# Whole weight blocks in fixed places, and a ring for their parts, in a two-layer trunk

## The chip, the core and the metric

The kernel runs on one core of a Trainium2 chip. A core has TensorE (matrix products, into the banks of PSUM), VectorE and ScalarE (elementwise work), GpSimd (called POOL in the profile) and SyncE, which here only issues transfers. Each engine works through its own queue in order; semaphores tie the queues together. The metric is the device time of one execution in microseconds (us): 1143.61 us for the kernel before, the median of three runs (1143.24 to 1144.23).

## The reference, cut to what matters

Two layers with RMS norms, 256 positions, width 2048, all in float32:

```python
# layer 0, gMLP
proj = xn @ w_in                       # 2048 -> 3 * 4096
u, v = split(gelu(proj[..., :8192])); zg = proj[..., 8192:]
v = rms_norm(v, v_g)
mixed = einsum('gts,bnsgc->bntgc', tril(w_s), v) + b_s
h = h + (u * mixed * silu(zg)) @ w_out # 4096 -> 2048
# layer 1, stick-breaking attention
q, k, v, zg = split(xn @ w_in)         # 2048 -> 4 * 2048
h = h + (attention(q, k, v) * silu(zg)) @ w_out
```

The weights are 218 MB in all.

## The kernel before

**A product of float32 numbers.** TensorE takes the operands as float32r. Each operand is cut into a high part (ScalarE's cast to float32r) and a low part (VectorE: the raw value minus the high part), and three matmuls, high x high, high x low and low x high, are added up in a bank (`terms`, L119 to L121). `cut` (L108 to L116) makes the parts of a weight tile: two weight rows of 128 x 512 at a time, so 1024 columns per operation, into tiles "hi" and "lo" of a pool of five.

**Seven products in place of eight.** The positions are two halves of 128, and the class `Pair` takes two blocks of 512 output columns together. Over the first `2 * ks` of the rows of 128 (`ks` is 4 or 5) it uses Winograd's form of Strassen's scheme: the weights make four blocks b11, b12, b21, b22, each of `ks` rows of 512 columns, and seven products p1 to p7 stand for eight. Sums of the left side (s1 to s4) are made once per layer (`sums`, `fifth`, `sums_of`); sums of the weight blocks are made for each pair on VectorE (`minus` at L284 to L286, and L314) or by transfers from GpSimd that add to what lies in SBUF (`plus`, L288 to L294). The other rows ("columns", `column`, L349 to L369) are multiplied plainly, with two rows and twelve matmuls per step.

A block's rows come in groups: two groups of two rows and, where `ks` is 5, a third group with the fifth row alone. Each group of 0 and 1 is a raw tile of its own (`load`, tags such as `b11_0`), so a block's sum is one VectorE operation per group, and each group has its own cut. The fifth rows lie elsewhere (`ex`, `wraw`).

**Order.** `head` emits p1 and p5, and a sum of b11 ahead of p5 (L308) and of p6 (L313, L314). `body` emits p6, p2, p7, p3 and p4, with a sum for p4 (L339), copies between banks (L326 to L338) and two additions of the fifth product `es` (L334, L342). In `run`, the column steps of the pair before are mixed between the groups of p1, p5 and p6. A scheduler with a model of the engines' times puts the instructions of each queue in their final order, so what is mixed in the trace may be mixed more finely than in the code.

There are 22 pairs: 3 named v, 8 gu, 2 o, 4 qk, 2 bv, 2 bg and 1 f. `ks` is 5 in two of the gu pairs, one o, three qk, and all bv, bg and f pairs.

**Names.** In the trace, `gu_p_hi` and `gu_p_lo` are the parts of a pair's block, `gu_hi` and `gu_lo` those of a column step, `gu_b` a raw block, and `gu_a` to `gu_e` the banks. Buffer numbers are left out.

Of the kernel before, what the change touches and what calls it, by code (L numbers as in the profile page):

```python
# [8 lines left out]
F32 = mybir.dt.float32  # L9
# [9 lines left out]
WARM = 9  # L19
KS_A = 4  # L20
# [9 lines left out]
def trunk_kernel(ctx: ExitStack, tc: tile.TileContext, x, xt, gcols, wst, wv0, a_w_in, a_v_norm_g,  # L30
# [29 lines left out]
    wspl = ctx.enter_context(tc.tile_pool(name="wspl", bufs=5))  # L60
# [45 lines left out]
    low = [None]  # L106

    def cut(raw, n, name, by=2):  # L108

        hi = wspl.tile([P, 2, CB], F32R, tag="hi", name=f"{name}_hi")  # L110
        lo = wspl.tile([P, 2, CB], F32R, tag="lo", name=f"{name}_lo")
        for i in range(0, n, by):
            sl = slice(i, min(i + by, n))
            nc.scalar.copy(hi[:, sl], raw[:, sl])  # L114
            low[0] = nc.vector.tensor_sub(lo[:, sl], raw[:, sl], f(hi[:, sl]))  # L115
        return hi, lo  # L116
# [6 lines left out]
    class Left:  # L123
# [10 lines left out]
        def sums(self, ks, out, name):  # L134

            for k0 in range(0, ks, 4):
                n = min(4, ks - k0)
                full = []
                for i in range(2):
                    sl = slice(i * ks + k0, i * ks + k0 + n)  # L140
                    fl = sraw.tile([P, 4, S], F32, tag=f"b1{i + 1}_1", name=f"{name}_full{i}{k0}")
# [4 lines left out]
                sm = [sraw.tile([P, 2, 4, P], F32, tag=f"b2{i + 1}_1", name=f"{name}_sm{i}{k0}") for i in range(2)]  # L146
# [3 lines left out]
                nc.vector.tensor_sub(s2, a11, s1)  # L150
                nc.vector.tensor_sub(s4, a12, s2)
                for i, si in enumerate((s1, s2, s3, s4)):
                    o = out[:, :, i, k0:k0 + n]
                    nc.scalar.copy(o[:, 0], si)
                    nc.vector.tensor_sub(o[:, 1], si, f(o[:, 0]))
            self.s, self.ks = [out], ks

        def fifth(self, out, name):
# [8 lines left out]
            nc.vector.tensor_sub(sm[:, 0], a21, a22)  # L167
            nc.vector.tensor_sub(sm[:, 1], a11, sm[:, 0])
# [6 lines left out]
        def sums_of(self, y, ks, out, name):  # L175
# [10 lines left out]
            nc.vector.tensor_sub(s24, a11, s13)  # L186
# [3 lines left out]
            nc.vector.tensor_sub(s24, a12, s24)  # L190
# [41 lines left out]

    class Pair:
# [3 lines left out]
        def __init__(self, src, left, nk, name, ks, evac, mid=None, fifth=None, fifth_first=False):  # L237
            self.fifth = fifth or (lambda j, name: ex.tile([P, 1, CB], F32, tag=f"b1{j + 1}_2", name=name))
            self.src, self.left, self.name, self.ks = src, left, name, ks
            self.evac, self.mid = evac, mid  # L240
# [8 lines left out]
        def load(self, i, j):  # L249
            tiles = {}  # L250
            for g in (range(len(self.groups)) if i else self.early):
# [4 lines left out]
                if g < 2:  # L256
                    raw = sraw.tile([P, n, CB], F32, tag=f"b{i + 1}{j + 1}_{g}", name=name)
# [4 lines left out]
            return [tiles[g] for g in sorted(tiles)]  # L262
# [21 lines left out]
        def minus(self, into, b0, b1, order=None):  # L284
            for g in order or range(len(self.groups)):
                nc.vector.tensor_sub(into[g], b0[g], b1[g])  # L286

        def plus(self, into, i, j, g0=0):  # L288

            for g in self.early:  # L290
                if g < g0:
                    continue
# [3 lines left out]
        def head(self):  # L296
# [11 lines left out]
            self.minus(self.b11, self.b12, self.b11, self.early)  # L308
# [4 lines left out]
            for g in range(len(self.b22)):  # L313
                nc.vector.tensor_add(self.b11[g], self.b22[g], self.b11[g])  # L314
            self.plus(self.b11, 1, 1, len(self.b22))

        def body(self, between=lambda: None):
# [10 lines left out]
            nc.scalar.copy(es, e)  # L328
            block(b11, lambda k: left.sum_part(1, k), b, "p6")
            c = self.bank("c")  # L330
# [8 lines left out]
            self.minus(b11, b21, b11)  # L339
# [110 lines left out]
    def load_x(i):  # L450

        xr.append(sraw.tile([P, XC, S], F32, tag=raws[i], name=f"xr{i}"))
# [5 lines left out]
    def load_h(c):  # L458

        hc.append(sraw.tile([P, NT, CB], F32, tag=("b11_1", "b12_1", "b21_1", "b22_1")[c], name=f"h0_{c}"))  # L460
# [192 lines left out]
    class YLeft(Left):  # L653
# [4 lines left out]
        def ready(self):  # L658

            full = [sraw.tile([P, 4, S], F32, tag=f"b21_{i}", name=f"so_full{i}") for i in range(2)]  # L660
# [446 lines left out]
    def mid_f(pair):  # L1107
# [5 lines left out]
        for k0, tag in zip(pair.rest[::2], ("b21_0", "b21_1", "b12_0", "b12_1")):  # L1113
            raw = sraw.tile([P, 2, CB], F32, tag=tag, name=f"fl_{k0}_raw")
# [81 lines left out]
```

## Time and profile before

| | |
|---|---|
| median of three runs | 1143.61 us |
| the profiled execution | 1143.29 us |
| its span, first to last instruction | 1141.6 us |
| mean granted TensorE clock | 0.999 |
| first weight matmul, end of the last | 5.09 us, 1134.3 us |
| VectorE, low parts of 1024 columns (gu pairs) | 112, mean 1222 ns |
| ScalarE, casts of 1024 columns (gu pairs) | 112, mean 1052 ns |
| transfers from HBM | 259.55 MB read |

A row of the timeline has the start, the duration, the engine, the line, the operation, the tiles (out <- in), the shape and the count; rows with a count above 1 are several operations in a row. A bracket gives the idle time before it and what ended it. A row of the list of groups has busy time and mean duration (ns) behind the first bar, and the engine's idle time before such operations behind the second. PE is TensorE, PEld its weight loads, DVE VectorE and ACT ScalarE.

### The profile page before, as it was taken

Reading aid. Unit: us, or ns where it says so; the run is one execution under the profiler, and the core shown is the slowest. Engines: PE = TensorE matmul, PEld = TensorE weight load, DVE = VectorE, ACT = ScalarE, POOL = GpSimd, SP = SyncE. Lnnn points to the kernel's source line nnn. Section 1 sums busy time; section 2 is a strip of 40 time slices with the busy share of each in tenths; the row PEclk is TensorE's granted clock in tenths of the full one; section 3 lists DMA queues with packets and bytes.
Section 4 is the critical chain, followed back from the end, with each engine's and each line's share of the span. In section 5 each row is a group of like instructions: output and inputs, shape, how many; then the busy total and the mean of one; then the engine's idle time right before and its main releaser. Section 6 shows DMA issues by size and latency. Waiting matters only on the chain.

```text
span 1141.6 us, 14838 instructions
## 1 busy us (share of the span) xinstructions
PE 1131.7 (99%) x5168; PEld 937.3 (82%) x5168; DVE 1011.4 (89%) x1111; ACT 830.4 (73%) x1102; POOL 91.4 (8%) x106
## 2 busy tenths in 40 slices
PE   9999999999999999999999999999999999999997
PEld 6888888888888888888888888888888888888886
DVE  7989889988998999978988787989989989897986
ACT  8676777777777778866657456788678887886564
POOL 0300110100110110100010000100100101000000
PEclk9999999999999999999999999999999999999999
DMA  9988788787787787685785877687687776837962
GB/s 348 329 269 277 215 243 272 198 257 246 186 266 256 189 262 241 175 291 140 264 259 167 293 200 277 146 279 214 176 288 195 210 232 175 270 87 241 350 205 88
DMA packets 79083, 264.72 MB, mean 232 GB/s; under 512 B 8992, under 2 KB 9504, under 8 KB 78880
## 3 DMA queue, kind: packets, MB, share of 16 engines
q1 hardware_dynamic: 67040, 227.57, 58.2%
q0 software_dynamic: 10672, 33.04, 15.9%
q10 hardware_dynamic: 1296, 3.17, 0.7%
q8 instruction: 40, 0.66, 0.2%
q14 instruction: 35, 0.29, 0.1%
HBM read 259.55 MB, written 4.19 MB: 231 GB/s over the span
## 4 chain that ended last, share of the span: by engine, by line
PE 93%; DMA 3%; ACT 1%; DVE 1%; issue 1%; SPq 0%; POOLq 0%; POOL 0%; ACTq 0%
PE gu_a L120 3%; PE gu_a L121 3%; PE gu_b L120 3%; PE gu_b L119 3%; PE gu_b L121 3%; PE gu_a L119 3%; PE op_acc L119 2%; PE op_acc L121 2%; PE op_acc L120 2%; PE gu_d L120 2%; PE gu_c L120 2%; PE gu_d L121 2%; PE gu_d L119 2%; PE gu_c L119 2%; PE gu_c L121 2%; PE qk_a L121 1%
## 5 line engine op out<-in xcount | busy, mean ns | idle before, releaser
L114 ACT CAST gu_p_hi<-gu_b 128x1024 fp32r<-128x1024 f32 (+1 forms) x126 | 123.1, 1004 | 37.0 <-PE gu_c L121 15.8
L115 DVE TENSOR_TENSOR gu_p_lo<-gu_b,gu_p_hi 128x1024 fp32r<-128x1024 f32 (+1 forms) x126 | 142.6, 1162 | 2.5 <-ACT gu_p_hi L114 2.0
L115 DVE TENSOR_TENSOR qk_p_lo<-qk_b,qk_p_hi 128x1024 fp32r<-128x1024 f32 (+1 forms) x77 | 80.7, 1073 | 10.0 <-ACT qk_p_hi L114 9.6
L114 ACT CAST qk_p_hi<-qk_b 128x1024 fp32r<-128x1024 f32 (+1 forms) x77 | 70.5, 934 | 22.3 <-PE o_c L121 3.7
L115 DVE TENSOR_TENSOR gu_lo<-gu_raw,gu_hi 128x1024 fp32r<-128x1024 f32 x60 | 72.0, 1217 | 7.8 <-ACT gu_hi L114 7.3
L114 ACT CAST gu_hi<-gu_raw 128x1024 fp32r<-128x1024 f32 x60 | 61.9, 1052 | 18.9 <-PE gu_d L121 8.6
L114 ACT CAST v_hi<-v_raw 128x1024 fp32r<-128x1024 f32 (+1 forms) x41 | 41.7, 1028 | 25.9 <-DMA v_raw<-in_a_w_in 21.7
L115 DVE TENSOR_TENSOR v_lo<-v_raw,v_hi 128x1024 fp32r<-128x1024 f32 (+1 forms) x41 | 48.8, 1193 | 13.1 <-ACT v_hi L114 12.7
L115 DVE TENSOR_TENSOR v_p_lo<-v_b,v_p_hi 128x1024 fp32r<-128x1024 f32 x42 | 50.3, 1220 | 4.8 <-ACT v_p_hi L114 4.6
L114 ACT CAST v_p_hi<-v_b 128x1024 fp32r<-128x1024 f32 x42 | 43.0, 1050 | 10.3 <-PE v_c L121 5.6
L115 DVE TENSOR_TENSOR bg_p_lo<-bg_b,bg_p_hi 128x1024 fp32r<-128x1024 f32 (+1 forms) x42 | 42.5, 1041 | 5.3 <-ACT bg_p_hi L114 5.1
L114 ACT CAST o_p_hi<-o_b 128x1024 fp32r<-128x1024 f32 (+1 forms) x35 | 33.4, 966 | 18.3 <-PE op_acc L121 13.0
L115 DVE TENSOR_TENSOR bv_p_lo<-bv_b,bv_p_hi 128x1024 fp32r<-128x1024 f32 (+1 forms) x42 | 42.5, 1040 | 3.7 <-ACT bv_p_hi L114 3.6
L114 ACT CAST bv_p_hi<-bv_b 128x1024 fp32r<-128x1024 f32 (+1 forms) x42 | 37.4, 908 | 9.3 <-PE qk_c L121 3.4
L114 ACT CAST bg_p_hi<-bg_b 128x1024 fp32r<-128x1024 f32 (+1 forms) x42 | 37.2, 907 | 8.6 <-PE bg_a L121 2.5
L115 DVE TENSOR_TENSOR o_p_lo<-o_b,o_p_hi 128x1024 fp32r<-128x1024 f32 (+1 forms) x35 | 38.3, 1113 | 5.4 <-ACT o_p_hi L114 5.4
L286 DVE TENSOR_TENSOR gu_b<-gu_b,gu_b 128x1024 f32<-128x1024 f32 (+1 forms) x36 | 41.7, 1174 | 0.1
L114 ACT CAST op_hi<-op_raw 128x1024 fp32r<-128x1024 f32 x24 | 25.1, 1053 | 19.9 <-PE op_acc L121 9.7
L114 ACT CAST o_hi<-o_raw 128x1024 fp32r<-128x1024 f32 x22 | 23.0, 1053 | 22.5 <-DMA o_raw<-in_a_w_out 15.8
L115 DVE TENSOR_TENSOR o_lo<-o_raw,o_hi 128x1024 fp32r<-128x1024 f32 x22 | 26.7, 1221 | 13.3 <-ACT o_hi L114 13.3
L120 PE MATMUL op_acc<-op_lo,yc 128*128 128x512 f32 x96 | 37.8, 393 | 0.0
L115 DVE TENSOR_TENSOR qk_lo<-qk_raw,qk_hi 128x1024 fp32r<-128x1024 f32 x26 | 31.4, 1219 | 7.2 <-ACT qk_hi L114 7.1
(798 smaller groups left out, 3778.8 us busy)
## 6 DMA issues: line engine op xcount, KB each, us to landing
gu_b<-in_a_w_in SPq DMA_DIRECT2D x64, 512.0 KB, 4.9
gu_raw<-in_a_w_in SPq DMA_DIRECT2D x60, 512.0 KB, 5.4
v_raw<-in_a_w_in SPq DMA_DIRECT2D x32, 512.0 KB, 5.5
qk_b<-in_b_w_in SPq DMA_DIRECT2D x32, 512.0 KB, 5.4
qk_raw<-in_b_w_in SPq DMA_DIRECT2D x26, 512.0 KB, 5.6
v_b<-in_a_w_in SPq DMA_DIRECT2D x24, 512.0 KB, 5.4
op_raw<-in_a_w_out SPq DMA_DIRECT2D x24, 512.0 KB, 4.6
o_raw<-in_a_w_out SPq DMA_DIRECT2D x22, 512.0 KB, 4.7
```

The costliest lines, as they stand in the source:

```text
L114: nc.scalar.copy(hi[:, sl], raw[:, sl])
L115: low[0] = nc.vector.tensor_sub(lo[:, sl], raw[:, sl], f(hi[:, sl]))
L119: nc.tensor.matmul(acc, lh, hi, start=first, stop=False, skip_group_check=True)
L120: nc.tensor.matmul(acc, lh, lo, start=False, stop=False, skip_group_check=True)
L121: nc.tensor.matmul(acc, ll, hi, start=False, stop=last, skip_group_check=True)
L286: nc.vector.tensor_sub(into[g], b0[g], b1[g])
```

## The change

The four raw blocks become four fixed tiles of four rows each (`quad`, 2048 columns), and the old tags are halves of them (`half_of`; `quarters` and `eighths` are other views of the same halves, for the tiles that shared the tags). Where a block has both groups, its sum is one VectorE operation over the whole tile, and so is its low part; the high part is still cast two rows at a time. The parts go to a ring of 12 places of 512 columns for each of hi and lo in place of five tiles of two; a block takes four places, a column step or a fifth row two, and a piece that doesn't fit before the end starts again at place 0. To write whole blocks in place, the signs of b11's sums are turned, and with them those of s1 and s2, of the fifth product's copy `es`, and of the sums for p4; the fifth rows keep the old signs with their own left sums. A new argument `far` is 0 in every pair, so its branches do nothing. The scratch for GpSimd's transfers is 8192 bytes. The number of matmuls and of transfers stays the same.

```diff
+SLOTS = 12
-    wspl = ctx.enter_context(tc.tile_pool(name="wspl", bufs=5))
+    wspl = ctx.enter_context(tc.tile_pool(name="wspl", bufs=1))
...
-    low = [None]
-    def cut(raw, n, name, by=2):
-        hi = wspl.tile([P, 2, CB], F32R, tag="hi", name=f"{name}_hi")
-        lo = wspl.tile([P, 2, CB], F32R, tag="lo", name=f"{name}_lo")
+    low, slot = [None], [0]
+    ring = [wspl.tile([P, SLOTS, CB], F32R, tag=nm, name=f"ring_{nm}") for nm in ("hi", "lo")]
+    quad = [[sraw.tile([P, 4, CB], F32, tag=f"b{i + 1}{j + 1}", name=f"b{i + 1}{j + 1}") for j in range(2)]
+            for i in range(2)]
+    def half_of(tag):
+        k = 2 * int(tag[4])
+        return quad[int(tag[1]) - 1][int(tag[2]) - 1][:, k:k + 2, :]
+    def cut(raw, n, name, by=2, low_by=4):
+        room = n + n % 2
+        if slot[0] + room > SLOTS:
+            slot[0] = 0
+        hi, lo = (r[:, slot[0]:slot[0] + n, :] for r in ring)
+        slot[0] += room
         for i in range(0, n, by):
             sl = slice(i, min(i + by, n))
             nc.scalar.copy(hi[:, sl], raw[:, sl])
+        for i in range(0, n, min(by, low_by) if by < 2 else low_by):
+            sl = slice(i, min(i + (by if by < 2 else low_by), n))
             low[0] = nc.vector.tensor_sub(lo[:, sl], raw[:, sl], f(hi[:, sl]))
...
         def block(self, b, part, acc, nm, first=False):
+            wide = None
             for g in order:
                 k0, n = self.groups[g]
-                hi, lo = cut(b[g], n, f"{self.name}_{nm}{g}")
+                if g >= 2:
+                    hi, lo = cut(b[g], n, f"{self.name}_{nm}{g}")
+                else:
+                    if wide is None:
+                        wide = cut(b.whole, 4, f"{self.name}_{nm}")
+                    hi, lo = (r[:, k0:k0 + n, :] for r in wide)
...
-            self.minus(self.b11, self.b12, self.b11, self.early)
+            for g in self.early:
+                if g >= 2:
+                    nc.vector.tensor_sub(self.b11[g], self.b12[g], self.b11[g])
+                elif g == 0:
+                    nc.vector.tensor_sub(self.b11.whole, self.b11.whole, self.b12.whole)
...
-            for g in range(len(self.b22)):
-                nc.vector.tensor_add(self.b11[g], self.b22[g], self.b11[g])
+            nc.vector.tensor_sub(self.b11.whole, self.b11.whole, self.b22.whole)
...
-            nc.scalar.copy(es, e)
+            nc.scalar.activation(es, e, AF.Identity, scale=-1.0)
...
-            self.minus(b11, b21, b11)
+            if self.far == 0:
+                nc.vector.tensor_add(b11.whole, b21.whole, b11.whole)
+            for g in range(self.far or 2, len(self.groups)):
+                (nc.vector.tensor_add if g < 2 else nc.vector.tensor_sub)(b11[g], b21[g], b11[g])
...
-    nc = bacc.Bacc("TRN2", target_bir_lowering=False, num_devices=1)
+    nc = bacc.Bacc("TRN2", target_bir_lowering=False, num_devices=1, dynamic_dma_scratch_size=8192)
```

More of the change, by code (lines that the diff above doesn't have):

```diff
@@ L261, in load @@
                 tiles[g] = raw
-            return [tiles[g] for g in sorted(tiles)]
+            block = Block(tiles[g] for g in sorted(tiles))
+            block.whole = quad[i][j]
+            return block
         def others(self, tiles, j):
@@ L282, in block, with plus @@
                 yield
[L284 to L288, printed above, removed]
+        def plus(self, into, i, j, g0=0, g1=9):
             for g in self.early:
-                if g < g0:
+                if not g0 <= g < g1:
                     continue
@@ L450, in load_x @@
     def load_x(i):
-        xr.append(sraw.tile([P, XC, S], F32, tag=raws[i], name=f"xr{i}"))
+        xr.append(quarters(raws[i]))
         if i > 0:
@@ L658, in ready @@
         def ready(self):
-            full = [sraw.tile([P, 4, S], F32, tag=f"b21_{i}", name=f"so_full{i}") for i in range(2)]
+            full = [quarters(f"b21_{i}") for i in range(2)]
             for i in range(2):
```

34 lines of the change are left out of this document (21 added, 13 removed).

## The prediction

> **What bounds the kernel now.** I read the page's engine table first, then the list of waits, then the stretches, and last single instructions.
>
> ```profile
> span 1141.6 us, 14838 instructions
> PE 1131.7 (99%) x5168; PEld 937.3 (82%) x5168; DVE 1011.4 (89%) x1111; ACT 830.4 (73%) x1102; POOL 91.4 (8%) x106
> ...
> PE 93%; DMA 3%; ACT 1%; DVE 1%; issue 1%; SPq 0%; POOLq 0%; POOL 0%; ACTq 0%
> ```
>
> TensorE is busy for 99% of the span and is 93% of the chain that ended last; VectorE, which the change relieves, is busy for 89% of it but only 1% of the chain. A busy matmul row need not be a matmul at full pace, so the pace comes next.
>
> ```profile
> 300.03 0.39 PE L120 MATMUL gu_c<-gu_lo,x_hi 128*128 128x512 f32 x1
> 300.26 0.39 PE L121 MATMUL gu_c<-gu_hi,x_lo 128*128 128x512 f32 x1
> 300.49 0.39 PE L120 MATMUL gu_e<-gu_p_lo,xs 128*128 128x512 f32 x1
> ```
>
> They start every 0.23 us though each lasts 0.39: this is the pipelined pace. The waits of TensorE over the whole span are these four and no more:
>
> ```profile
> PE wps L79 <- DVE warm L76: 1.3, 1, 1.3
> PE v_acc L119 <- ACT v_hi L114: 0.7, 1, 0.7
> PE v_c L119 <- ACT v_c L331: 0.4, 1, 0.4
> PE gT L430 <- ACT bsg L1006: 0.2, 1, 0.2
> ```
>
> By stretch (columns: stretch, its length, then busy time of PE, PEld, DVE, ACT, POOL; the last three are the clock granted to TensorE, the DMA share and GB/s):
>
> ```profile
> 5.00:62.00 57.00, 56.01 (x241) 44.83 (x240) 50.86 (x60) 45.65 (x77) 9.27 (x5) 1.00 0.98 354
> 62.00:190.00 128.00, 127.87 (x564) 105.90 (x565) 116.03 (x121) 93.53 (x125) 11.23 (x15) 1.00 0.80 249
> 190.00:485.00 295.00, 295.00 (x1304) 244.25 (x1303) 275.20 (x281) 228.37 (x272) 31.27 (x32) 1.00 0.76 230
> 720.00:1050.00 330.00, 329.81 (x1596) 276.52 (x1595) 297.46 (x324) 261.86 (x362) 24.71 (x29) 1.00 0.72 212
> 1134.40:1141.60 7.20, 0.00 (x0) 0.00 (x0) 1.36 (x3) 1.97 (x4) 0.55 (x1) 0.80 0.64 236
> ```
>
> From 62 us to the last matmul TensorE does not stop and its clock is full. What could be won by a faster VectorE is therefore the part of the first stretch that is lost (57.00 - 56.01 = 1.0 us), 0.1 us in the second and 0.2 us near 1028: about 1.3 us. The last 7.2 us (squares, root, stores) are untouched.
>
> **The change, part by part.**
>
> Merged VectorE operations first. The rows by shape:
>
> ```profile
> L115 DVE TENSOR_TENSOR gu_p_lo<-gu_b,gu_p_hi 128x1024 fp32r<-128x1024 f32 x112 | 134.4, 1222 | 2.5 <-ACT gu_p_hi L114 2.0
> L286 DVE TENSOR_TENSOR gu_b<-gu_b,gu_b 128x1024 f32<-128x1024 f32 x32 | 39.1, 1236 | 0.1
> L314 DVE TENSOR_TENSOR gu_b<-gu_b,gu_b 128x1024 f32<-128x1024 f32 x16 | 19.3, 1216 | 0.0
> L115 DVE TENSOR_TENSOR gu_p_lo<-gu_b,gu_p_hi 128x512 fp32r<-128x512 f32 x14 | 9.5, 681 | 0.0
> ```
>
> The eight gu pairs show 14 low parts, 4 + 2 block sums of 1024 columns each. A pair thus loses 7 + 3 = 10 operations, and the program has 22 pairs (3 v, 8 gu, 2 o, 4 qk, 2 bv, 2 bg, 1 f): 220 fewer. From 512 to 1024 columns the duration grows by 1222 - 681 = 541 ns, so 2048 columns are estimated at 1222 + 2 x 541 = 2304 ns, 140 ns less than two of 1222: 31 us less busy time at most. Operations without a wait overlap, however:
>
> ```profile
> 243.64 1.22 DVE L286 TENSOR_TENSOR gu_b<-gu_b,gu_b 128x1024 f32<-128x1024 f32 x1
> 244.78 1.22 DVE L115 TENSOR_TENSOR gu_p_lo<-gu_b,gu_p_hi 128x1024 fp32r<-128x1024 f32 x1
> 245.91 1.22 DVE L115 TENSOR_TENSOR gu_lo<-gu_raw,gu_hi 128x1024 fp32r<-128x1024 f32 x1
> ```
>
> They start 1.13 us apart, so two of them hold VectorE for 2.27 us against 2.304 - 0.09 = 2.21 for the merged one: 0.06 us a merge, 13 us in all. I take 13 us (0.6 us a pair), with 0 and 31 as bounds. [...]
>
> By the waits above none of this is on the path; it is worth 0 to 1.3 us to the end, and I take 0.4, the size of the one wait that falls among a pair's blocks (v_c); the losses before it lie ahead of the first pair.
>
> What is added is **lateness**. A low part now waits for both casts of its block and comes out whole. Where VectorE is the busy engine, the first half of a block is ready 2.21 - 1.13 = 1.08 us later, the second no later. Does TensorE have that time? Thin and middling cases, VectorE's row above, the first matmul that reads it below:
>
> ```profile
> 933.78 1.22 DVE L115 TENSOR_TENSOR qk_p_lo<-qk_b,qk_p_hi 128x1024 fp32r<-128x1024 f32 x1
> ...
> 935.54 0.39 PE L120 MATMUL qk_d<-qk_p_lo,x 128*128 128x512 f32 x1
> ```
>
> ```profile
> 729.72 1.22 DVE L115 TENSOR_TENSOR bv_p_lo<-bv_b,bv_p_hi 128x1024 fp32r<-128x1024 f32 x1
> ...
> 732.48 0.39 PE L120 MATMUL bv_b<-bv_p_lo,xs 128*128 128x512 f32 x1
> ```
>
> ```profile
> 63.09 1.23 DVE L115 TENSOR_TENSOR v_p_lo<-v_b,v_p_hi 128x1024 fp32r<-128x1024 f32 x1 [0.25 <-ACT v_p_hi L114]
> ...
> 65.20 0.39 PE L120 MATMUL v_b<-v_p_lo,xs 128*128 128x512 f32 x1
> ```
>
> They lead by 935.54 - 935.00 = 0.54, by 1.54 and by 0.88 us. Matched in order in the same way through the whole trace, the first of these is the thinnest of the 154 blocks of the pairs, half lead by some 3 us or more, and four by less than 1.08: the 0.54 and 0.88 above and two just under it. These four would be short by 0.54 + 0.20 + 0.1 + 0.1 = 0.9 us. I take 0.9; the bounds are 0 (earlier merges of the pair repay 0.06 each, and other matmuls can be placed ahead) and the next part's.
>
> The sums make a longer chain in blocks p5 and p6: whole sum (+1.08), second cast, whole low part (+1.08). The cast:
>
> ```profile
> L114 ACT CAST gu_p_hi<-gu_b 128x1024 fp32r<-128x1024 f32 x112 | 115.4, 1052 | 34.9 <-PE gu_c L121 15.2 <-DVE gu_b L314 13.0 <-issue 3.7
> ```
>
> So the first half of p5 can come 1.08 + 1.05 + 1.08 = 3.2 us later, but only where VectorE has nothing else to do in those 2.1 us of casts; in p5 and p6 it has the column blocks' low parts (1.13 each) and TensorE has their matmuls, so I take 0 there, and keep up to 1.65 us (3.2 less the 1.54 above) per pair for the rival below.
>
> The first pair (v2) is the exception, since its weights arrive late (DMA share 0.98 above):
>
> ```profile
> 33.31 1.05 ACT L114 CAST v_p_hi<-v_b 128x1024 fp32r<-128x1024 f32 x1
> ...
> 38.76 1.04 ACT L114 CAST v_p_hi<-v_b 128x1024 fp32r<-128x1024 f32 x1
> ...
> 40.06 0.39 PE L120 MATMUL v_a<-v_p_lo,x_hi 128*128 128x512 f32 x1
> ```
>
> The second cast of its p1 ends at 39.80, a whole low part at 39.80 + 2.30 = 42.1, and TensorE wanted the first half at 40.06. Column matmuls can go ahead for one step; a loss of 0 to 2.0 us stays. I take 0.7.
>
> The **ring** of 12 replaces 5 tiles of 2. A fifth block takes two places, so a five-tile pair's block takes 6 and the ring holds two blocks. When TensorE has finished a block's four, the matmuls ahead of the block after next are a fifth, a four and a fifth: (3 + 12 + 3) x 0.227 = 4.08 us, and the last cast and the whole low part take 1.05 + 2.30 = 3.35, which leaves 0.7 us. Before, four of five tiles remained (4.08 to 4.76 us) against 1.05 + 1.22: 1.8 to 2.5 us. In four-tile pairs the ring holds three blocks and leaves 5.44 - 3.35 = 2.1 us. I take 0, since the leads of p3 and p4 were already mostly near 2 us; the price if not is the first rival.
>
> Signs of the sums, fixed places instead of fresh tiles and the negated copy of the fifth bank keep their instruction counts: 0, but for that copy, which goes from a COPY to an ACTIVATE:
>
> ```profile
> L328 ACT COPY gu_es<-gu_e 128x512 f32<-128x512 f32 x8 | 4.7, 589 | 2.0 <-PE gu_e L121 2.0
> L851 ACT ACTIVATE q<-qk_a,r2q 128x512 f32<-128x512 f32 x4 | 2.8, 691 | 4.0 <-PE qk_a L121 4.0
> ```
>
> That is 0.1 us for each of 22 on ScalarE, which is 73% busy: 0 on the path. The loads into b11 wait for the whole low part of p4 instead of half of it; three or four column blocks (12 matmuls each, 2.7 us) and p4's own lie between it and the next p1, so 0. The smaller scratch bears on POOL's transfers, of which a pair has two or three at a time:
>
> ```profile
> gu_b<-in_a_w_in POOLq DMA_DIRECT2D x16, 512.0 KB, 6.9
> ```
>
> I take 0. If one had to wait for the landing of another, it would come 6.9 us later, and p7, which reads it, comes after p5, p6 and p2 (36 matmuls or more, 8.2 us).
>
> Sum: -0.4 + 0.9 + 0.7 = **+1.2 us** on the profiled execution's 1143.29 us (its span of 1141.6 and 1.7 around it); the median is 1143.61, so I forecast **1144.8 us**.
>
> **The rivals.**
>
> *Slower: the ring is too short in the five-tile pairs.* Eleven pairs have five (2 gu, 1 o, 3 qk, 2 bv, 2 bg, 1 f). In p7, p3 and p4 the margin is 0.7 us, and any VectorE operation that comes between two low parts, such as the sums with es, uses it up:
>
> ```profile
> 309.38 0.69 DVE L334 TENSOR_TENSOR gu_b<-gu_b,gu_es 128x512 f32<-128x512 f32 x1
> ```
>
> From there on TensorE waits. VectorE and ScalarE serve their queues in order, so everything behind the waiting low part is late as well. At 0.2 us a block, 33 blocks give 6.6 us, minus what was counted already: about 1150; with p5 and p6 short too (1.65 us in a few pairs), up to 1156. For it: VectorE at 297.46 of 330 us in that stretch. Against it: no wait of TensorE there now, though leads fall to 0.54. It decides from the point where VectorE's other work between two low parts exceeds the 0.7 us.
>
> *Faster: VectorE's relief reaches TensorE.* At most the 1.3 us found above and some 1 us of matmuls that start later after a semaphore: 1141.3 or little below. Against it: nearly no waits to remove.
>
> *It doesn't do what it says*: if slices of the ring are tracked as one tile, every cast waits for all matmuls, some 3 us for each of 154 blocks, over 1500 us. The kernel already writes its x parts in slices of one tile while matmuls read others, which speaks against it.
>
> **How the numbers follow.** Forecast 0.54 (1143 to 1145.9), ring too short 0.38 (1146 to 1156), faster 0.06 (1140 to 1141.3), not as said 0.02. What a measurement here can tell from no change is 0.2%, 2.3 us: 1141.3 to 1145.9. So faster 0.06, same 0.54, slower 0.40. The range 1141.8 to 1151 leaves out the faster case, the last and the top of the first rival; the forecast's own is 1143 to 1145.9.
>
> **What would show it.** Right: rows of 128x2048 near 2300 ns, 220 fewer VectorE instructions, VectorE busy some 13 to 31 us less, TensorE still busy from 62 us on. Ring too short: waits of TensorE for low parts in qk, bv and bg, and of ScalarE's casts for matmuls. Wrong altogether: a different matmul pace from 0.23 us, or a gain of over 2.3 us, which would need matmuls that went away.

## The result, and the profile after

The changed kernel takes 1213.0 us (median of four runs, 1211.76 to 1217.54) against 1143.55 us (1143.24 to 1144.23) for the kernel before on the same chip: a ratio of 1.061, with a 95% interval of 1.0592 to 1.0629. It is 69 us slower, far outside the predicted range of 1141.8 to 1151. The parts below go by what the loss consists of, what was tried, and which step of the prediction failed.

First the page of the changed kernel: its span, the busy times, the chain that ended last.

```profile
span 1210.1 us, 14458 instructions
...
PE 1156.6 (96%) x5168; PEld 942.9 (78%) x5168; DVE 994.7 (82%) x891; ACT 823.7 (68%) x1101; POOL 87.4 (7%) x106
...
PE 5%; DMA 3%; DVE 3%; issue 2%; ACT 2%; POOLq 0%; POOL 0%; ACTq 0%; DVEq 0%
```

VectorE has 891 instructions in place of 1111, 220 fewer, and is busy for 16.7 us less, as forecast. Of the chain that ended last only some 15% of the span could be followed this time, so its shares say little against the 93% of TensorE before. The busy times say more: TensorE was idle for 9.9 us of the span before (1141.6 - 1131.7) and is idle for 53.5 us now, 43.6 us more, and it is counted as busy 24.9 us longer for the same 5168 matmuls. The groups of the long pieces (line, engine, operation, tiles, shape, count; busy us and mean ns; idle time before them and its releaser):

```profile
L135 DVE TENSOR_TENSOR ring_lo<-b,ring_hi 128x2048 fp32r<-128x2048 f32 (+1 forms) x157 | 354.8, 2269 | 99.6 <-ACT ring_hi L132 98.8
...
L132 ACT CAST ring_hi<-b 128x1024 fp32r<-128x1024 f32 x311 | 316.8, 1049 | 145.3 <-DMA b<-in_a_w_in 29.7
```

A low part of 2048 columns takes 2.3 us, as estimated. But VectorE, the engine that was to be relieved, stands idle for 99.6 us ahead of these operations, nearly all of it for ScalarE's casts. By stretch, with the columns of the prediction (length, busy PE, PEld, DVE, ACT, POOL; clock granted to TensorE, DMA share, GB/s):

```profile
62.00:190.00 128.00, 124.38 (x542) 100.96 (x541) 108.67 (x84) 87.53 (x117) 11.17 (x14) 1.00 0.72 238
190.00:547.00 357.00, 336.48 (x1459) 272.59 (x1458) 294.73 (x238) 245.81 (x297) 26.88 (x33) 0.99 0.68 217
715.00:1050.00 335.00, 321.69 (x1486) 264.22 (x1485) 276.38 (x236) 239.44 (x339) 24.88 (x29) 0.97 0.68 211
```

Before, TensorE was busy for nearly the whole of such stretches (127.87 of 128.00, 295.00 of 295.00 and 329.81 of 330.00 us). Now it lacks 3.6, 20.5 and 13.3 us in them, so the loss is spread over nearly the whole kernel and is not one accident. Some of it does not show as idle time: the clock is below 1.00 in two of them, 0.99 and 0.97 (the last section comes back to this). At the head of TensorE's list of waits (total us, times, longest; some 45 us in all) stand two kinds of places, low parts of p2 (`gu_a`) and casts for p6 (the `b` banks):

```profile
PE gu_a L140 <- DVE ring_lo L135: 7.5, 6, 1.7
PE qk_b L139 <- ACT ring_hi L132: 6.1, 4, 2.6
PE gu_b L139 <- ACT ring_hi L132: 5.9, 4, 3.8
PE bg_b L139 <- ACT ring_hi L132: 4.2, 2, 2.1
```

One such stall in a gu pair of four rows, in VectorE's timeline from p1's low part on (start, duration; brackets: idle time and what ended it):

```profile
245.97 2.29 DVE L135 TENSOR_TENSOR ring_lo<-b,ring_hi 128x2048 fp32r<-128x2048 f32 x1 [3.04 <-ACT ring_hi L132]
...
249.32 2.29 DVE L341 TENSOR_TENSOR b<-b,b 128x2048 f32<-128x2048 f32 x1
...
258.62 2.29 DVE L135 TENSOR_TENSOR ring_lo<-b,ring_hi 128x2048 fp32r<-128x2048 f32 x1 [0.22 <-ACT ring_hi L132]
263.13 1.23 DVE L135 TENSOR_TENSOR ring_lo<-gu_raw,ring_hi 128x1024 fp32r<-128x1024 f32 x1 [2.21 <-ACT ring_hi L132]
264.27 2.28 DVE L346 TENSOR_TENSOR b<-b,b 128x2048 f32<-128x2048 f32 x1
268.67 2.29 DVE L135 TENSOR_TENSOR ring_lo<-b,ring_hi 128x2048 fp32r<-128x2048 f32 x1 [2.12 <-ACT ring_hi L132]
271.00 2.29 DVE L373 TENSOR_TENSOR b<-b,b 128x2048 f32<-128x2048 f32 x1
273.21 2.29 DVE L135 TENSOR_TENSOR ring_lo<-b,ring_hi 128x2048 fp32r<-128x2048 f32 x1
```

These are p1's low part, the sum for p5, p5's low part, a column step's, the sum for p6, p6's low part, the sum for p4, and p2's low part. Each link can start only behind the one before it: the sum overwrites b11, so it waits for the low part, the casts wait for the sum, and the low part waits for both casts. Other work of the two queues stands between them too: the column step's low part at 263.13 waited for its cast and stands ahead of the sum for p6. From the end of p1's low part (248.26) to the end of p6's (270.96) pass 22.7 us. TensorE meanwhile:

```profile
271.00 0.39 PE L139 MATMUL gu_b<-ring_hi,xs 128*128 128x512 f32 x1
...
273.72 0.39 PE L141 MATMUL gu_b<-ring_hi,xs 128*128 128x512 f32 x1
275.55 0.50 PE L140 MATMUL gu_a<-ring_lo,x_hi 128*128 128x512 f32 x1 [1.44 <-DVE ring_lo L135]
```

p6 (`gu_b<-ring_hi,xs`) starts at 271.00, as soon as its low part is there, with no column step left beside it, and 2.7 us later p2's low part, two pieces of 2.29 us behind p6's on VectorE, is not there. With pieces in halves (the run halves_all below) p6's low part is there at 258.26 in the same pair, and p6 starts at 263.91, 5.6 us later; here the lead is 0.04 us.

### The profile page after: what moved, and what is told of

The parts are those of the page before. It is cut to its first block, busy times and chain, and to the rows that moved or that the text cites. A ratio compares the mean times of both kernels' runs of the same rounds, so it can differ in the third digit from the quotient of the medians.

```text
span 1210.1 us, 14458 instructions
## 1 busy us (share of the span) xinstructions
PE 1156.6 (96%) x5168; PEld 942.9 (78%) x5168; DVE 994.7 (82%) x891; ACT 823.7 (68%) x1101; POOL 87.4 (7%) x106
## 5 line engine op out<-in xcount | busy, mean ns | idle before, releaser
L135 DVE TENSOR_TENSOR ring_lo<-b,ring_hi 128x2048 fp32r<-128x2048 f32 (+1 forms) x157 | 354.8, 2269 | 99.6 <-ACT ring_hi L132 98.8
L132 ACT CAST ring_hi<-b 128x1024 fp32r<-128x1024 f32 x311 | 316.8, 1049 | 145.3 <-DMA b<-in_a_w_in 29.7
L135 DVE TENSOR_TENSOR ring_lo<-gu_raw,ring_hi 128x1024 fp32r<-128x1024 f32 x60 | 72.0, 1219 | 14.5 <-ACT ring_hi L132 14.3
L132 ACT CAST ring_hi<-gu_raw 128x1024 fp32r<-128x1024 f32 x60 | 61.6, 1051 | 31.8 <-DMA gu_raw<-in_a_w_in 23.5
L140 PE MATMUL gu_a<-ring_lo,x_hi 128*128 128x512 f32 x128 | 51.4, 402 | 7.5 <-DVE ring_lo L135 7.5
L135 DVE TENSOR_TENSOR ring_lo<-v_raw,ring_hi 128x1024 fp32r<-128x1024 f32 (+1 forms) x41 | 48.6, 1193 | 5.3 <-ACT ring_hi L132 5.2
L373 DVE TENSOR_TENSOR b<-b,b 128x2048 f32<-128x2048 f32 x22 | 50.3, 2288 | 0.4
L141 PE MATMUL gu_a<-ring_hi,x_lo 128*128 128x512 f32 x128 | 50.5, 395 | 0.0
L341 DVE TENSOR_TENSOR b<-b,b 128x2048 f32<-128x2048 f32 x22 | 50.3, 2284 | 0.2 <-DMA b<-in_a_w_in 0.2
L139 PE MATMUL gu_a<-ring_hi,x_hi 128*128 128x512 f32 x128 | 50.4, 394 | 0.0
L346 DVE TENSOR_TENSOR b<-b,b 128x2048 f32<-128x2048 f32 x22 | 50.3, 2285 | 0.1
L132 ACT CAST ring_hi<-o_raw 128x1024 fp32r<-128x1024 f32 x22 | 22.9, 1052 | 24.9 <-DMA o_raw<-in_a_w_out 19.6
L141 PE MATMUL op_acc<-ring_hi,yc 128*128 128x512 f32 x96 | 37.5, 393 | 0.0
L139 PE MATMUL op_acc<-ring_hi,yc 128*128 128x512 f32 x96 | 36.3, 395 | 0.3 <-ACT yc L605 0.3
```

Of the source, the lines that this page charges most:

```text
L139: nc.tensor.matmul(acc, lh, hi, start=first, stop=False, skip_group_check=True)
L140: nc.tensor.matmul(acc, lh, lo, start=False, stop=False, skip_group_check=True)
L141: nc.tensor.matmul(acc, ll, hi, start=False, stop=last, skip_group_check=True)
L341: nc.vector.tensor_sub(self.b11.whole, self.b11.whole, self.b12.whole)
L346: nc.vector.tensor_sub(self.b11.whole, self.b11.whole, self.b22.whole)
L373: nc.vector.tensor_add(b11.whole, b21.whole, b11.whole)
```

## The experiments

Each group was put on record with its expectations before it ran. Medians are in us; a ratio is to the kernel before on the same chip, with its 95% interval. All edits are to the changed kernel unless said otherwise.

### Which part of the change costs

Four edits: pieces back to 1024 columns, with ring, fixed places, signs and scratch as changed; either kind of piece alone; and two orders that looked bad in the trace.

```diff
 # halves_all, low_halves: a low part behind each cast
             nc.scalar.copy(hi[:, sl], raw[:, sl])
-        for i in range(0, n, min(by, low_by) if by < 2 else low_by):
-            sl = slice(i, min(i + (by if by < 2 else low_by), n))
             low[0] = nc.vector.tensor_sub(lo[:, sl], raw[:, sl], f(hi[:, sl]))
 # halves_all, sum_halves: all three sums in two operations, as here
-            nc.vector.tensor_sub(self.b11.whole, self.b11.whole, self.b22.whole)
+            for g in range(2):
+                nc.vector.tensor_sub(self.b11[g], self.b11[g], self.b22[g])
 # fifth_and_sum_late: p4's sum behind p7's low part; likewise
 # the fifth row's cut behind the casts of its block in p6, p2, p7, p3, p4
+                with tc.issue_after(ins_of(low[0])):
                     nc.vector.tensor_add(b11.whole, b21.whole, b11.whole)
```

> The changed kernel with its ring of 12, its fixed places, its signs and the small scratch, but with every low part and every block sum in two VectorE operations of 1024 columns again. Theory G (the price is in the pieces of 2048 columns, which come whole and late, and in the orders that the scheduler makes of them): back to about 1144 us, within 1140 to 1150. Theory R (the price is in the ring, the fixed places or the scratch: a cast waits for a place, a load for a whole block): stays over 1190 us.

> Only the low parts in operations of 1024 columns; the three block sums stay whole. Theory G: the whole sums alone still keep p6 late, so part of the loss stays: 1165 to 1190 us if the sums carry as much as the lows. Theory R: over 1190 us as before.

> Only the block sums in operations of 1024 columns; the low parts stay whole. Theory G: 1160 to 1190 us, and together with the run of whole sums the two losses should add up to about the 69 us of the change if they are independent. Theory R: over 1190 us.

> The changed kernel with two orders set by hand: in p6, p2, p7, p3 and p4 the cast of the fifth row stands behind the casts of the block's four on ScalarE, and the sum for p4 stands behind p7's low part on VectorE. The operations are the same. Theory O (the loss is made by two places in the queues: a cast of the fifth row that waits up to 7 us for an accumulating transfer with p6's casts behind it, and a whole sum of 2.3 us ahead of p2's low part): about 65 us of waits less their rest, 1145 to 1165 us. Theory G without the orders (it is the lateness of the pieces themselves): over 1185 us.

| run | low parts | sums | us | ratio |
|---|---|---|---|---|
| halves_all | 1024 | 1024 | 1144.96 | 1.0007 [0.9995, 1.0018] |
| low_halves | 1024 | 2048 | 1152.27 | 1.007 [1.0045, 1.0096] |
| sum_halves | 2048 | 1024 | 1194.83 | 1.0433 [1.0333, 1.0532] |
| changed | 2048 | 2048 | 1213.0 | 1.061 [1.0592, 1.0629] |
| fifth_and_sum_late | 2048 | 2048 | 1200.22 | 1.048 [1.0449, 1.0511] |

With halves the loss is gone, so ring, fixed places, signs and scratch cost nothing that can be measured. Whole sums alone cost 7 us, whole low parts alone 50, both 68: they make each other worse. (Theory G had expected 1165 to 1190 and 1160 to 1190 for the two, so its even shares were wrong.) The two orders account for 13 us; they can't be the main cause.

### Which blocks

Low parts whole in some blocks only, with sums in halves; then one sum left out, on the chain or off it (part of the computation is then missing).

```diff
 # chain_whole: WHOLE = ("p1", "p5", "p6"); rest_whole: ("p2", "p7", "p3", "p4")
-                        wide = cut(b.whole, 4, f"{self.name}_{nm}")
+                        wide = cut(b.whole, 4, f"{self.name}_{nm}", low_by=4 if nm in WHOLE else 2)
 # no_p6_sum
-            nc.vector.tensor_sub(self.b11.whole, self.b11.whole, self.b22.whole)
 # no_p4_sum
-            if self.far == 0:
-                nc.vector.tensor_add(b11.whole, b21.whole, b11.whole)
```

> Low parts whole in p1, p5 and p6 alone, in halves in p2, p7, p3 and p4; sums in halves, all else as in the changed kernel. Whole low parts in all seven blocks gave 1194.8 us, none 1145.0, so 50 us are to be shared out. Theory C (the chain: p5 and p6 wait for a sum of the block before, two casts and a whole low part in a row, TensorE spends the column steps meanwhile, and what follows has no lead left): most of it, 1180 to 1195. Theory P (each block with a whole low part is late by itself, wherever it stands): 3 of 7 blocks, 50 x 3/7 = 21 us, 1160 to 1172. Theory Q (the late pieces are those that stand one behind another on VectorE after the columns are gone, p2's, p7's, p3's and p4's): little, 1145 to 1155.

> The other half of that: low parts whole in p2, p7, p3 and p4 alone. Theory C: little, 1145 to 1160. Theory P: 4 of 7 blocks, 28 us, 1168 to 1178. Theory Q: most of it, 1180 to 1195.

> The changed kernel without the sum of b11 and b22 for p6, so p6 takes the block of p5 once more (part of the computation is left out). It takes 22 VectorE operations of 2.3 us away, and p6's casts no longer wait for p5's low part and the sum. Theory C (the chain through p5 and p6): most of the loss goes, 1145 to 1175. Theory V (VectorE is simply too full of long pieces, wherever they stand): the same as without p4's sum, 1185 to 1205.

> The changed kernel without the sum of b11 and b21 for p4 (part of the computation is left out; p4 takes b11 as its transfer leaves it). The same 22 operations of 2.3 us less on VectorE, off the chain from p1 to p6. Theory C: only what stood ahead of p2's low part is won, 1195 to 1213. Theory V: as without p6's sum, and no less than half of the loss, 1185 or below.

| run | us | ratio |
|---|---|---|
| chain_whole | 1176.29 | 1.0284 [1.0246, 1.0321] |
| rest_whole | 1153.99 | 1.0089 [1.0059, 1.0118] |
| no_p6_sum | 1169.20 | 1.0217 [1.0181, 1.0252] |
| no_p4_sum | 1205.22 | 1.0531 [1.0491, 1.0572] |

Three whole blocks on the chain cost 31 us more than halves, four off it 9; by numbers of blocks it would have been 21 and 28. Taking 22 operations of 2.3 us off VectorE wins 44 us where they stand on the chain and 8 where they don't. So it is not VectorE's load, and not a long piece as such. chain_whole came out just below its theory's 1180: the rest of the 50 us needs both sets at once.

### The order of the queues, or the pieces

The scheduler orders the queues by a model, and whole pieces change its answer: in several gu pairs more of the last column steps are mixed with p6's first matmuls when pieces are halves (in the pair shown above p6 stands behind all of them in both). Two runs exchange TensorE's orders (a list of 4695 places, taken from the other program, chains the weight matmuls); two change what is written first.

```diff
 # whole_halves_order (changed kernel), halves_whole_order (halves_all)
+    seq = [ins_of(mms[i + m - 128]) for i, m in enumerate(moved)]
+    for a, b in zip(seq, seq[1:]):
+        tc.add_manual_dep(b, a.name, NOSYNC, reason="order of matmuls")
 # sums_first: the sum for p6 behind p5's cut (for p5 behind p1's)
                         wide = cut(b.whole, 4, f"{self.name}_{nm}")
+                        if then is not None:
+                            then()
 # columns_spread
-        steps = (3 if len(pair.groups) > 2 else 2) * len(pair.groups)
+        steps = 3 * len(pair.groups)
```

> The changed kernel, its 4695 weight matmuls held to the order that they have in the kernel with low parts and sums in halves (1145.0 us). The orders of VectorE and ScalarE stay the scheduler's. Theory S (the loss is in the order that the scheduler gave TensorE: all columns ahead of p6, none left as cover for it; the pieces themselves would be in time): 1145 to 1160. Theory D (the whole pieces are themselves late; the other order is only the scheduler's answer to it): 1180 or more, and above 1213 if that answer was a good one.

> The fourth corner: low parts and sums in halves, the weight matmuls held to the order of the changed kernel. Theory S (the order is what costs): 1185 to 1215, since p6 again has no columns beside it. Theory D (the whole pieces are what costs): 1145 to 1160, since every piece is there sooner than this order asks for it.

> The changed kernel, with the whole sum for p5 written right behind p1's cut and the one for p6 right behind p5's cut, so that the scheduler sees them ahead of the column steps' low parts. Theory C1 (the chain from p1 to p6 is late mostly because VectorE's queue puts column low parts, which wait for transfers, ahead of the sums: 263.13 ahead of 264.27 in the changed kernel): some 3 us in each of about 14 pairs are won, 1170 to 1195. Theory C2 (the chain is late by the durations of its own links, whole sum, two casts, whole low part, twice): no more than 10 us, 1200 to 1215.

> The changed kernel, with the column steps of the pair before spread over p1, p5 and p6 in all pairs, where four-tile pairs have them between the groups of p1 and p5 alone. Theory C (p6 comes late by the chain and there is no column left beside it): the stalls of the four-tile pairs shrink, 1175 to 1200. If the columns are not what is missing (the pieces behind p6 come too slowly whatever TensorE does ahead of them): 1205 to 1220.

| run | us | ratio |
|---|---|---|
| whole_halves_order | 1211.45 | 1.0591 [1.056, 1.0622] |
| halves_whole_order | 1157.94 | 1.0123 [1.0094, 1.0153] |
| sums_first | 1210.39 | 1.0577 [1.0544, 1.0609] |
| columns_spread | 1205.97 | 1.0538 [1.048, 1.0596] |

In either order of TensorE whole pieces take 1211 to 1213 us, and halves 1145 to 1158. The pieces themselves are late; the order is 13 us at most. Column steps kept for p6 gain some 7 us, about the least that its interval tells from none and less than the theory of missing cover asked for, and earlier sums nothing that their intervals tell from none. What is wrong lies deeper than the queues' order.

### A loop through b11

b11 serves p1, p5, p6 and p4, and its next load waits for p4's low part. If this loop set the pair's period, cutting it should give nearly everything back. The sum for p4 goes to b21, which is free by then; the same was done to low_halves, halves_all and sums_first.

```diff
-                nc.vector.tensor_add(b11.whole, b21.whole, b11.whole)
+                nc.vector.tensor_add(b21.whole, b21.whole, b11.whole)
...
-            block(b11, lambda k: left.part(HALVES[1][k], 1), d, "p4")
+            b4 = Block(b21[:2] + b11[2:])
+            b4.whole = b21.whole
+            block(b4, lambda k: left.part(HALVES[1][k], 1), d, "p4")
```

> The changed kernel, with p4's sum written into b21 in place of b11, so that b11 is free for the next pair's load when that sum is done, and not when p4's low part is (in the changed kernel 273.3 us against 283.8 us in the pair looked at). All pieces stay whole, and the number of instructions stays the same. Theory L (a loop through b11: load, p1, two sums, p6, p4, load, some 5 us longer per pair than with halves; the pair's period is the time once round): cutting some 10 us out of it brings TensorE's own time back, 1144 to 1165. Theory N (no loop; p6 is late by the chain's length, measured from whatever p1 starts after, and b11's load is held by the queue of loads anyway): 1195 to 1215.

> The same edit with low parts and sums in halves (1145.0 us without it). Theory L: with halves the loop just fits TensorE's time, so at most the few us of stalls that are left can go: 1141.5 to 1145. Theory N: 1144 to 1146.

> The same edit with low parts in halves and whole sums (1152.3 us without it). Theory L: 1142 to 1147. Theory N: 1149 to 1153.

> The same edit with all pieces whole and the sums for p5 and p6 written right behind the cuts (1210.4 us without the edit). Theory L: as p4_in_b21 or up to 10 us better, since order can matter once the loop is cut. Theory N: 1195 to 1212.

| run | with p4 in b21 | ratio | without |
|---|---|---|---|
| p4_in_b21 | 1212.64 | 1.0601 [1.0585, 1.0617] | 1213.0 |
| halves_p4_in_b21 | 1145.58 | 1.0015 [1.0006, 1.0024] | 1144.96 |
| lowhalves_p4_in_b21 | 1158.70 | 1.0128 [1.0115, 1.0141] | 1152.27 |
| sums_first_p4_in_b21 | 1212.92 | 1.0601 [1.0588, 1.0615] | 1210.39 |

The theory of the loop fell: nothing is won, and low_halves loses 6 us. But the trace of p4_in_b21 shows what waits in its place. ScalarE's timeline, p1's two casts in the same gu pair:

```profile
247.24 1.06 ACT L132 CAST ring_hi<-b 128x1024 fp32r<-128x1024 f32 x1 [2.37 <-PE gu_d L141]
248.64 1.05 ACT L132 CAST ring_hi<-b 128x1024 fp32r<-128x1024 f32 x1 [0.35 <-PE gu_d L141]
```

In the changed kernel it waited for its transfer:

```profile
243.35 1.05 ACT L132 CAST ring_hi<-b 128x1024 fp32r<-128x1024 f32 x1 [3.30 <-DMA b<-in_a_w_in]
```

With b11 free earlier the block is there, and the cast waits for TensorE, for matmuls into `gu_d`. That is p4 of the pair before, and p4 holds the places that p1 needs: the twelve places handed out before p1 went to p4 (4) and to the four steps of column 0 (8), so p1 gets p4's. The two releases are 1.40 us apart, which is the time of six matmuls, half of p4 (these start 0.227 us apart in this trace; 6 x 0.227 = 1.36).

### The ring as a window

By the same count p5's first two places come free when TensorE has done the last but one step of column 0 of the pair before, and the other two when it has done the last one, 12 matmuls or 2.7 us later. A whole low part needs both. So the ring of 12 would be the window that the longer chain no longer fits into. A ring of 14 places was tried up to the end of the gu pairs; to make room for it these all have four rows and the mixing weights one buffer, and gu12 has the same with 12 places.

```diff
 # gu12 and gu14
-KS_GU = (4, 4, 4, 5, 4, 5, 4, 4)
+KS_GU = (4,) * 8
-        pb = lg.enter_context(tc.tile_pool(name="pb", bufs=2))
+        pb = lg.enter_context(tc.tile_pool(name="pb", bufs=1))
     pv.close()
+    lr.close()
+    wspl = lr.enter_context(tc.tile_pool(name="wspl2", bufs=1, side="right"))
+    slot[0], slots[0] = 0, 12
+    ring[:] = [wspl.tile([P, 12, CB], F32R, tag=nm, name=f"ring_{nm}") for nm in ("hi", "lo")]
 # gu14 alone
-SLOTS = 12
+SLOTS = 14
```

> The control for the next run: the changed kernel with all eight gu pairs at four rows (two had five), one buffer in place of two for the mixing weights, and the ring of 12 laid down anew after the gu pairs; this makes room in SBUF. All theories: about the changed kernel's 1213 us, 1205 to 1220, since two five-tile pairs less take their stalls with them and the rest costs a few us.

> The same with a ring of 14 places up to the end of the gu pairs (3 v and 8 gu), of 12 behind them. Theory W (the ring is the window: p1's and p5's casts can't run before TensorE has given back places, as the casts at 247.24 us show when b11 comes early, and the longer chain of whole pieces no longer fits into 12 places): two places are a column step, 2.7 us, in each of 11 pairs, so 12 to 30 us less than the control. Theory M (the window is not what holds the chain; transfers and the queues of ScalarE and VectorE do): within 4 us of the control.

gu12 takes 1205.51 us (1204.8 to 1207.97), ratio 1.0537 [1.0519, 1.0555]; gu14 1188.04 us (1186.27 to 1191.31), ratio 1.039 [1.0367, 1.0412]. Two places won 17.5 us, within theory W's 12 to 30. The stretches show that they were won where the ring is longer. First gu12, then gu14, then halves_all (with its two five-row gu pairs), each from the first gu matmul to the last, and from there to the last matmul of the f pair:

```profile
164.80:543.40 378.60, 363.56 (x1572) 292.45 (x1572) 309.41 (x243) 260.50 (x315) 27.83 (x35) 1.00 0.66 213
543.40:1197.90 654.50, 637.00 (x2923) 520.65 (x2921) 542.05 (x516) 440.14 (x605) 41.78 (x47) 0.99 0.67 207
```

```profile
160.80:524.20 363.40, 360.87 (x1583) 294.44 (x1582) 309.33 (x244) 261.76 (x316) 32.84 (x35) 1.00 0.68 217
524.20:1176.80 652.60, 637.27 (x2922) 520.59 (x2921) 541.97 (x516) 440.53 (x605) 41.90 (x47) 0.99 0.67 210
```

```profile
160.90:513.50 352.60, 352.21 (x1565) 291.00 (x1565) 321.30 (x333) 268.64 (x327) 73.24 (x38) 1.00 0.77 233
513.50:1136.30 622.80, 621.53 (x2923) 518.30 (x2921) 544.35 (x622) 439.27 (x603) 38.17 (x47) 1.00 0.71 216
```

Against halves_all the gu pairs end 29.9 us late in gu12 (543.4 - 513.5) and 10.7 us late in gu14 (524.2): two thirds of the loss there is gone with every piece still whole. Behind them, where both rings have 12 places, both take the same time, some 30 us more than with halves. How it comes about is seen in ScalarE's rows of gu12, p5's casts in the same gu pair:

```profile
253.82 1.05 ACT L133 CAST ring_hi<-b 128x1024 fp32r<-128x1024 f32 x1 [1.10 <-PE gu_d L142]
255.64 1.05 ACT L133 CAST ring_hi<-gu_raw 128x1024 fp32r<-128x1024 f32 x1 [0.78 <-PE gu_a L142]
256.71 1.28 ACT L658 ACT_TABLE_LOAD   x1
258.01 0.69 ACT L658 ACTIVATE g<-gu_a,n_r 128x512 f32<-128x512 f32 x1
258.60 0.68 ACT L658 ACTIVATE g<-gu_d,n_r 128x512 f32<-128x512 f32 x1
259.17 1.04 ACT L133 CAST ring_hi<-b 128x1024 fp32r<-128x1024 f32 x1
```

The first cast waits for TensorE; the second stands behind a column's cast, which waits for TensorE too, and behind the activations that read the finished banks of column 0. It comes 5.4 us after the first, and the whole low part with it. In gu14 the two are one row, released by the sum for p5:

```profile
250.35 2.00 ACT L133 CAST ring_hi<-b 128x1024 fp32r<-128x1024 f32 x2 [1.50 <-DVE b L342]
```

VectorE's rows of p1's and p6's low parts, gu12 and then gu14:

```profile
247.27 2.29 DVE L136 TENSOR_TENSOR ring_lo<-b,ring_hi 128x2048 fp32r<-128x2048 f32 x1 [2.95 <-ACT ring_hi L133]
...
269.94 2.29 DVE L136 TENSOR_TENSOR ring_lo<-b,ring_hi 128x2048 fp32r<-128x2048 f32 x1 [2.12 <-ACT ring_hi L133]
```

```profile
244.61 2.29 DVE L136 TENSOR_TENSOR ring_lo<-b,ring_hi 128x2048 fp32r<-128x2048 f32 x1 [0.20 <-ACT ring_hi L133]
...
261.51 2.29 DVE L136 TENSOR_TENSOR ring_lo<-b,ring_hi 128x2048 fp32r<-128x2048 f32 x1 [0.93 <-ACT ring_hi L133]
```

From one to the other pass 22.7 us with 12 places, as in the changed kernel, and 16.9 us with 14. This pair is one of the best: over the eight gu pairs the means are 22.1 us with 12 places, 18.9 us with 14, and 16.7 us in halves_all.

## Why the prediction was wrong

**What bounds the kernel** was read rightly: TensorE, with some 1.3 us to be won. So the gain was limited to nothing, and the loss was the whole question.

**Merged operations**: right in count (220), mean duration (2284 to 2290 ns for 2304) and near in busy time (16.7 us less for 13); the 0.4 us that it was to win at the end can't be seen beside the loss. Fewer and longer operations did save VectorE time, and cost the kernel four times as much (69 us for 16.7).

**Lateness, +0.9 us: this step failed.** It took the leads of single blocks in the trace of before and subtracted 1.08 us from each, as if every block were late by its own piece and by nothing else. But a lead is what is left after a chain, and in p1, p5 and p6 each late piece starts the next one later. It also took the second half of a block as no later than before. With whole pieces the first half is as late as the second; and the second half's cast can be several us behind the first (253.82 and 259.17), which a low part in halves does not mind, since the first half's is made meanwhile.

**The chain, +3.2 us, taken as 0 because the column steps cover it: this is the larger mistake.** In the pair looked at p6's low part ends 22.7 us after p1's; in halves_all it is earlier. VectorE's rows in halves_all, p1's second half and p6's second half (with p2's first half in the same row):

```profile
237.77 1.22 DVE L133 TENSOR_TENSOR ring_lo<-b,ring_hi 128x1024 fp32r<-128x1024 f32 x1 [1.68 <-ACT ring_hi L132]
...
257.04 2.58 DVE L133 TENSOR_TENSOR ring_lo<-b,ring_hi 128x1024 fp32r<-128x1024 f32 x2
```

From 238.99 to 258.26 pass 19.3 us, 3.4 us less. Measured in the same way in the 21 pairs behind the first, the means are 20.9 and 17.7 us, 3.2 us apart, and 22 times that is 70 us, about what was lost. Both agreements are partly chance. The 3.2 us of the prediction were for the first half of p5 alone, these are for the whole way from p1's low part to p6's; and the means by kind of pair differ, 4.0 us in the gu pairs against 1.3 us in the two v pairs, with nothing in the first pair. What failed is the cover. Column steps keep TensorE busy, but they are work that has to be done anyway: what they cover in one pair is only free if the chain starts earlier by as much in the next. In the v and gu pairs it can't, because the ring lets ScalarE run no more than 12 places ahead of TensorE, so a lead that is used up is not made up again. (That the ring holds it there is shown by the two places more; that a lead is never made up is argued, from the loss that grows pair by pair.) Taking p6's sum out of the chain (44 us won) and lengthening the window by two places (19 us won in half of the pairs) show the two sides of this.

**The ring, taken as 0, and the rival that it is too short in the five-tile pairs (1146 to 1156).** Right in the part, wrong in the place. It is too short, but only for whole pieces: with halves it costs nothing. And not where the prediction looked, in p7, p3 and p4 of eleven pairs at 0.2 us a block, but ahead of p1 and p5, in four-row pairs too, where its places come free with the column steps of the pair before. rest_whole, with whole low parts in p2, p7, p3 and p4, loses 9 us, near the 6.6 us that the rival gave for these blocks, but not where it said: its last gu matmul ends 7.0 us behind that of halves_all (520.9 against 513.9) and its last f matmul 7.8 us (1144.5 against 1136.7), so the stretch with nine of the eleven five-row pairs loses under 1 us. The size agrees by luck.

**Loads into b11, taken as 0**: right in what they cost, not in the reason given. p1's first cast does wait for its load (3.30 us above); but when the load comes earlier (p4_in_b21) nothing is won, since the places of the ring are next. **Signs, fixed places, scratch, the negated copy**: 0, as halves_all shows. **The first pair**, +0.7: not tried alone; from 5 to 62 us TensorE is busy for 55.73 us against 56.01 before and 55.46 in halves_all, so no price of whole pieces is seen there.

**Of what would show it**, the waits of TensorE for low parts in qk, bg and bv (3.2, 0.6 and 0.6 us), named for the short ring, appeared, and those in gu are larger; the pace of matmuls, named as a sign that all was wrong, did change in places (0.43 us in place of 0.23, below).

What stays open: the 10.7 us that are left in the gu pairs with 14 places, and what holds the pairs of the second layer, where a longer ring was not tried. There the chain counts too: in chain_whole the last gu matmul ends 8.7 us behind that of halves_all and the last f matmul 28.2 us. In p6 of the five-row pairs ScalarE's queue has the fifth row's cast, which waits for a transfer that adds, ahead of the block's other two:

```profile
867.75 0.62 ACT L132 CAST ring_hi<-qk_b 128x512 fp32r<-128x512 f32 x1 [7.37 <-DMA qk_b<-in_b_w_in]
868.27 1.99 ACT L132 CAST ring_hi<-b 128x1024 fp32r<-128x1024 f32 x2
```

fifth_and_sum_late moved it together with p4's sum (13 us for both); the two were not parted. No version that was run is faster than the kernel before, whose TensorE has nearly no waits left to be freed from; halves_all is level with it.

## What to carry to other kernels

A piece's size is a matter of latency as much as of cost: before two operations are merged, follow the chain in which they stand (who waits for the whole that could have gone on with a half) and add it up link by link, and don't take work as cover unless the chain can also start earlier. A ring of buffers is a window in time: count how many places back each piece's predecessor lies, and when its last user is done, and do so for the whole piece, since the last place to come free now counts for all of it. And a lead measured in the old trace says little once the order and the chain have changed.

## What the runs showed of the hardware

In the changed kernel's trace the matmuls themselves became slow after stretches with few of them: 0.43 us from start to start in place of 0.23. TensorE's timeline in a qk pair of five rows:

```profile
866.41 0.39 PE L141 MATMUL qk_c<-ring_hi,x 128*128 128x512 f32 x1
869.36 0.50 PE L139 MATMUL qk_b<-ring_hi,xs 128*128 128x512 f32 x1 [2.56 <-ACT ring_hi L132]
871.25 0.50 PE L139 MATMUL qk_b<-ring_hi,x 128*128 128x512 f32 x1 [1.40 <-ACT ring_hi L132]
...
873.23 0.63 PE L141 MATMUL qk_b<-ring_hi,xs 128*128 128x512 f32 x1
873.65 0.63 PE L139 MATMUL qk_b<-ring_hi,xs 128*128 128x512 f32 x1
874.08 0.63 PE L140 MATMUL qk_b<-ring_lo,xs 128*128 128x512 f32 x1
...
878.77 0.40 PE L139 MATMUL qk_a<-ring_hi,x 128*128 128x512 f32 x1
879.01 0.40 PE L140 MATMUL qk_b<-ring_lo,x 128*128 128x512 f32 x1
```

And the stretches of this place and of another like it, each with the 3.41 us ahead of it:

```profile
868.53:871.94 3.41, 1.18 (x3) 0.48 (x3) 2.90 (x3) 3.41 (x6) 0.00 (x0) 1.00 0.00 0
871.94:878.77 6.83, 6.18 (x15) 4.79 (x15) 6.83 (x6) 3.32 (x5) 0.00 (x0) 0.50 0.25 77
820.75:824.16 3.41, 1.56 (x7) 1.00 (x6) 2.85 (x2) 3.41 (x7) 0.00 (x0) 1.00 0.00 0
824.16:827.58 3.42, 3.42 (x9) 2.65 (x9) 3.42 (x2) 2.97 (x5) 0.00 (x0) 0.50 0.00 0
```

After some 6 us with a few matmuls (866.4 to 872.6), the next 13 start 0.43 us apart in place of 0.23, with a granted clock of 0.50, and TensorE counts as busy meanwhile (6.18 of 6.83 us). So a stall of 6 us cost another 13 x 0.2 = 2.6 us behind it. Behind the first 5 us, 58 matmuls of the trace start 0.38 to 0.47 us after the one before (2 in the trace of the kernel before), which at 0.2 us each makes up to 11 us of the 69, and none of them is in a list of waits.

It took no long stall: in the 3.41 us ahead of 824.16 TensorE had one wait, of 1.85 us. Up to the last weight matmul the trace has six stretches at half clock, 3.41 or 6.83 us long, and they start whole multiples of 3.41 us apart (411.15, 421.39, 824.16, 871.94, 1018.72 and 1073.33). In the 3.41 us ahead of each TensorE was busy for 0.5 to 1.64 us; the least busy of the other slots of 3.41 us counted off in this way, with 1.67 us (506.72 to 510.13), was not followed by half clock. So in this trace half clock came behind each slot in which TensorE was busy for 1.64 us or less, and behind none with 1.67 or more, but for the second halves of the stretches of 6.83. Where a wait fell made a difference: the 1.85 us ahead of 824.16 lay within one slot, while a wait of 1.86 us (229.80 to 231.66) was split between two, which kept 2.97 and 1.99 us of busy time, and the clock stayed at 1.00. That it is the busy time of a slot that decides is inferred from this one trace.
